# Attention scores of a pair of heads as 64-row products issued in turn into two banks

## The chip, the core and the metric

The kernel runs on one core of one Trainium2 chip. The metric is device time in microseconds (us) of one execution. Before the change it is 724.13 us, the median of three runs (723.54 to 724.2). The engines named below are TensorE (PE, with its weight loads as PEld), VectorE (DVE), ScalarE (ACT) and SyncE (SP), which issues the DMAs.

## The reference

One layer of a hybrid block over 512 latent tokens (a grid of 8 rows by 64 columns) and 256 context tokens, 1024 wide, 16 heads of 64. The change lies in branch B, a neighbourhood attention with all context keys in one softmax:

```python
s_nb = (jnp.einsum('bqhd,bpqjhd->bqhpj', q_r, k_win).astype(jnp.float32) * scale
        + jnp.transpose(bias, (1, 0, 2, 3))[None].astype(jnp.float32))
s_ctx = jnp.einsum('bqhd,bchd->bqhc', q_r, k_ctx).astype(jnp.float32) * scale
p = jax.nn.softmax(jnp.concatenate([s_nb, s_ctx], axis=-1), axis=-1).astype(v.dtype)
```

A score is a sum over the 64 channels of one head. Branch A (a gated short convolution), the projections, the gates, the merge and the output projection stand around it.

## The kernel before

All matrix operands are kept as two parts of type fp32r, a high part H (the rounded value) and a low part L (what rounding left), and a product of two matrices is a sum of three products, H·H + H·L + L·H (`step_T`, L115 to L117). `split` (L70, L71) makes the parts: the cast of H on ACT, the difference L on DVE.

The tokens are ordered by grid column, so that 512 queries fall into four blocks of 128, and a block's window keys are at most 256 of the 512 latent keys. With 256 context keys a block of one head has 512 scores, one bank of PSUM. Heads go in eight pairs (`p`); a pair fills 128 partitions, its first head the lower 64 (`lo`), its second the upper 64 (`hi`).

`keys_queries(p)` projects a pair's queries and keys and makes their parts. As a head has 64 channels only, the parts are doubled: for head h, `qd[h]` holds the high part of its queries in both halves of the partitions and `qe[h]` the low part in both; `ks[h]` holds the high part of its keys in its own half and the low part in the other. A product with 128 rows of `qd[h]` with `ks[h]` is then H·H + H·L, one of `qe[h]` with `ks[h]` is L·H + L·L. So `scores(p, h, b)` needs two products of 512 columns for a block (L552), or four of 256 in block 3, whose window keys lie apart (L561). It then adds the bias and takes the maximum on DVE (L568), the exponential with its sum on ACT (L574), the reciprocal (L575) and the scaling (L576).

`turn2` transposes the probabilities of two blocks of one head on PE (L583) and splits them into TH and TL. `gather(p, h, TH, TL)` multiplies them with the values (L599) and writes a head's 64 rows of `attn[p]`.

These steps are laid between projections that the rest of the layer needs: `plan` gives each pair its list, as generators that yield after 16 to 32 products. The last loop runs over 64 blocks (p, h, b); at each it takes the next pieces of fill, issues a finished head's gather, and issues the scores two blocks ahead. What stands in which order on an engine is then settled by a scheduler, which keeps to this order by and large.

Of eight PSUM banks the fill has three, the scores two (`psS`, one block each), the transposes two, the gather one. `bt` holds the bias of the two heads, loaded by SP at a head's first block; the 512 KB halves of the weight chunks (`raw`) go through the same queue. The last pieces are the gather of the last head and `gate2(3)`; after them the merge stage splits the conv branch (`us`) and the attention (`as`) and multiplies them with their output weights.

Of the kernel before, what the change touches and what calls it, by code (L numbers as in the profile page):

```python
# [9 lines left out]
F32 = mybir.dt.float32  # L10
F32R = mybir.dt.float32r
AF = mybir.ActivationFunctionType
ALU = mybir.AluOpType
AX = mybir.AxisListType

P = 128
D = 1024
KT = 8
S = 512
C = 256  # L20
EPS = 1e-6
NPAIR = 8
# [5 lines left out]
def layer(ctx: ExitStack, tc, xp, ctxt, ctxT, cc, wmod, small, wfirst, win, wout, wo, rel, tab, out):  # L28
    nc = tc.nc
# [25 lines left out]
    def pairs(tag, n, dtype=F32R):  # L55
        t = [hp.tile([P, 2, n], dtype, name=f"{tag}{k}") for k in range(KT)]
        return t, ([x[:, 0] for x in t], [x[:, 1] for x in t])
# [6 lines left out]
    _, hx = pairs("h", S)  # L64
    hcs, hc = pairs("hc", C)

    def split(H, L, src, scale=None):

        if scale is None:
            nc.scalar.copy(H, src)  # L70
            nc.vector.tensor_sub(L, src, H.bitcast(F32))  # L71
        else:
            nc.scalar.mul(H, src, scale)
            nc.vector.scalar_tensor_tensor(
                out=L, in0=src, scalar=scale, in1=H.bitcast(F32), op0=ALU.mult, op1=ALU.subtract
            )
# [152 lines left out]
    def unit(w, i, m=hx):  # L229
        ps = pj()  # L230
        proj_T(ps, w, i, m)
        return ps


    with ExitStack() as p0:
# [8 lines left out]
        tps = Banks(6, 7)  # L244
# [8 lines left out]
        cols = {}  # L253
# [61 lines left out]
        with tc.manual_schedule(engines={E.PE, E.DVE, E.Activation, E.SP}):  # L315
# [74 lines left out]
            for k in range(KT):  # L390
# [9 lines left out]
                m = st.tile([P, S], F32, name="m", bufs=2)  # L400
# [57 lines left out]
        ks = [5, 6, 7, 0, 1, 2, 3, 4]  # L458
# [13 lines left out]
    aw = pa.enter_context(tc.tile_pool(name="aw", bufs=2, reuse_waits="tile"))  # L472
    swap = [(i + 16) % 32 for i in range(32)]
    lo, hi = slice(0, 64), slice(64, P)
    psS, psT, psO = Banks(3, 4), Banks(5, 6), Banks(7)
    bt = aw.tile([P, 5, 256], F32, name="bt", bufs=1)
    nc.vector.memset(bt[:, 4], 0.0)
    V, KQ = {}, {}
# [30 lines left out]
    def keys_queries(p):  # L509
        w = chunk()  # L510
        qf = rope(unit(w, 0), 64)
        sc = 0.125
        qd = [aw.tile([P, S], F32R, name="qd", bufs=3) for h in range(2)]
        qe = [aw.tile([P, S], F32R, name="qe", bufs=3) for h in range(2)]
        for h, r in ((0, lo), (1, hi)):
            for o in (lo, hi):
                nc.scalar.mul(qd[h][o], qf[r], sc)  # L517
            for o in (lo, hi):
                nc.vector.scalar_tensor_tensor(
                    out=qe[h][o], in0=qf[r], scalar=sc, in1=qd[h][r].bitcast(F32), op0=ALU.mult, op1=ALU.subtract  # L520
                )
            if h == 0:
                yield
        ks = [aw.tile([P, S + C], F32R, name="ks", bufs=4) for h in range(2)]

        def keys(src, cols):
            for h, r, o in ((0, lo, hi), (1, hi, lo)):
                nc.scalar.copy(ks[h][r, cols], src[r])
                nc.vector.tensor_sub(ks[h][o, cols], src[r], ks[h][r, cols].bitcast(F32))

        keys(rope(unit(w, 1)), slice(0, S))
        yield
        ps = pj()
        proj_c(ps, w, 1)
        keys(summed(ps), slice(S, S + C))
        KQ[p] = qd, qe, ks
        yield

    def scores(p, h, b):
        qd, qe, ks = KQ[p]
        if b == 0:
            nc.sync.dma_start(bt[:, 2 * h:2 * h + 2], rel[p, h])
        s = psS()
        qs = slice(b * P, (b + 1) * P)
        if b < 3:

            t = ks[h][:, b * P:(b + 2) * P]
            kt = bass.AP(t.tensor, t.offset, [t.ap[0], [(4 - b) * P, 2], [1, 2 * P]])  # L550
            for n, lhs in enumerate((qd[h], qe[h])):
                nc.tensor.matmul(  # L552
                    s.rearrange("p (a c) -> p a c", a=2), lhsT=lhs[:, qs], rhs=kt, start=n == 0, stop=n == 1
                )
        else:
            kt = ks[h].rearrange("p (t c) -> p t c", c=P)
            s4 = s.rearrange("p (t c) -> p t c", c=P)
            n = 0
            for lhs in (qd[h], qe[h]):
                for o, i in ((slice(0, 2), slice(0, 4, 3)), (slice(2, 4), slice(4, 6))):  # L560
                    nc.tensor.matmul(  # L561
                        s4[:, o], lhsT=lhs[:, qs], rhs=kt[:, i], start=n == 0, stop=n == 3, skip_group_check=True
                    )
                    n += 1
        e = 2 * h + (b == 3)
        m = aw.tile([P, 1], F32, name="m", bufs=4)
        s3 = s.rearrange("p (a c) -> p a c", a=2)
        nc.vector.tensor_tensor_reduce(  # L568
            out=s3, in0=s3, in1=bt[:, e::4 - e][:, 0:2], scale=-1.0, scalar=3.0e38,
            op0=ALU.add, op1=ALU.min, accum_out=m,  # L570
        )
        pt = aw.tile([P, S], F32, name="pt", bufs=3)
        z = aw.tile([P, 1], F32, name="z", bufs=4)
        nc.scalar.activation(pt, s, AF.Exp, bias=m, scale=-1.0, accum_out=z)  # L574
        nc.vector.reciprocal(z, z)  # L575
        nc.scalar.mul(pt, pt, z)  # L576
        return pt

    def turn2(pts, b, TH, TL):
        tps = [psT().rearrange("p (c q) -> p c q", c=4) for _ in pts]  # L580
        for tp, pt in zip(tps, pts):
            for c in range(4):
                nc.tensor.transpose(tp[:, c], pt[:, c * P:(c + 1) * P], ident)  # L583
        for n, tp in enumerate(tps):
            split(TH[:, b + n], TL[:, b + n], tp)

    def gather(p, h, TH, TL):
        r, q = (lo, hi)[h], (hi, lo)[h]
        o = psO()
        o3 = o.rearrange("p (b q) -> p b q", b=4)  # L590

        work = [(4, slice(0, 4), lambda t: t[:, :, 2]), (5, slice(0, 4), lambda t: t[:, :, 3])]
        work.append((0, slice(0, 4, 3), lambda t: t[:, 0:4:3, 0]))
        for k in range(1, 3):
            work.append((k, slice(k - 1, k + 1), lambda t, k=k: t.rearrange("p b c q -> p (b c) q")[:, 4 * k - 3:4 * k + 1:3]))
        work.append((3, slice(2, 4), lambda t: t[:, 2:4, 1]))
        for n, (kt, dst, src) in enumerate(work):
            for t in (TH, TL):
                nc.tensor.matmul(  # L599
                    o3[:, dst], lhsT=V[p][:, kt, h], rhs=src(t),  # L600
                    start=n == 0 and t is TH, stop=n == len(work) - 1 and t is TL,
                )
        tmp = aw.tile([P, S], F32, name="tmp", bufs=1)
        nc.scalar.copy(tmp[r], o[q])
        nc.vector.tensor_add(attn[p][r, 64:512], o[r, :448], tmp[r, :448])
        nc.vector.tensor_add(attn[p][r, 0:64], o[r, 448:], tmp[r, 448:])
# [10 lines left out]
    def gate2(g):  # L617
        w = chunk()
        gate(2 * g, w, 0)
        yield  # L620
        gate(2 * g + 1, w, 1)
        yield
# [13 lines left out]
    def chain(*gs):  # L636
        for g in gs:
            yield from g
# [11 lines left out]
    for p in range(NPAIR):  # L650
        f = []
# [5 lines left out]
            }[name](i))  # L657
        fill.append(f)
    pj.tags = (0, 1, 2)
    blocks = [(p, h, b) for p in range(NPAIR) for h in range(2) for b in range(4)]  # L660
    pts = {n: scores(*blocks[n]) for n in range(2)}
    T = None
    done = 0
    for i, (p, h, b) in enumerate(blocks):
        slot = i % 8
        if slot == 0:
            items = chain(*(g for g, _ in fill[p]))
            total, done = sum(n for _, n in fill[p]), 0
        upto = -(-total * (slot + 1) // 8)
        while done < upto:  # L670
            next(items)
            done += 1
        if T is not None and b == 0:
            gather(*T)
        if i + 2 < len(blocks):
            pts[i + 2] = scores(*blocks[i + 2])
        if b == 0:
            TH = aw.tile([P, 4, 4, P], F32R, name="TH", bufs=1)
            TL = aw.tile([P, 4, 4, P], F32R, name="TL", bufs=1)
            T = p, h, TH, TL  # L680

        if b % 2:
            turn2([pts.pop(i - 1), pts.pop(i)], b - 1, TH, TL)
    gather(*T)
    for _ in gate2(3):
        pass
    pa.close()

# [4 lines left out]
    for n, srcs in (("u", u), ("a", attn)):  # L693
        t = [bp.tile([P, 2, S], F32R, name=f"{n}s{k}") for k in range(KT)]
# [48 lines left out]
    for j in range(KT):  # L743
        w = chunk()
        g = G[j]
        for i in range(2):
            nc.vector.scalar_tensor_tensor(  # L747
                out=g[i], in0=g[i], scalar=1.0, in1=unit(w, i, ua[i]), op0=ALU.add, op1=ALU.mult
# [8 lines left out]
        if j == 1 or j == 3:  # L757
            q = j // 2
# [9 lines left out]
        if j == 4:  # L768
# [4 lines left out]
            for i in range(2):  # L773
                gb = cv.tile([P, S], F32, name="ta")
                ps = pj()
                for k in range(4):
                    n = 4 * i + k
# [91 lines left out]
    for q in range(2):  # L869
        nc.vector.scalar_tensor_tensor(  # L870
            out=raws[q][:, :, h0], in0=raws[q][:, :, h0], scalar=-1.0, in1=raws[2 + q][:, :, h0],
            op0=ALU.mult, op1=ALU.subtract,
        )
        split(S4[q][:, 0], S4[q][:, 1], raws[q][:, :, h0])
    t = [hp.tile([P, 2, S], F32R, name=f"wB22{i}", tag=f"h{2 + i}") for i in range(4)]
# [25 lines left out]
    for i in range(2):  # L901
        cols = slice(256 * i, 256 * (i + 1))
# [92 lines left out]
```

## Time and profile before

| | |
|---|---|
| median of three runs | 724.13 us |
| the profiled execution, its time | 723.86 us |
| its span (first to last instruction) | 722.1 us |
| PE clock granted over the span | 0.999 |
| score products | 96 of 512 columns (L552), 64 of 256 (L561) |
| other products in the stage of the scores | transposes 256 (L583), gathers 192 (L599), the rest projections |
| DMA over the span | 86.63 MB, 120 GB/s |

The stage from the first score to the last gather lies between about 137 and 515 us of the span. In the rows shown later, a group's line gives the kernel's line, the engine, the operation, the tile written and those read, the shapes and the count, then busy time and mean duration in ns, and last the idle time of the engine before the group and what ended it. In a timeline a row has its start, its length and, in brackets, idle time and what ended it. A matmul's duration runs until its last result is written, and the next one starts earlier; so sums of durations are not time, and distances of starts are.

### The profile page before, as it was taken

The page shows a single profiled execution, that of the slowest core. Times are in us where ns is not written, and L with a number is a line of the kernel's source. Part 1 is how long each engine was busy: PE and PEld are TensorE (multiplying, and loading weights), DVE is VectorE, ACT ScalarE, POOL GpSimd, SP SyncE. Part 2 cuts the span into 40 slices and gives each one's busy share as a digit, 9 for nine tenths or more (in the row PEclk, how much of TensorE's full clock was granted, in tenths as well). Part 3 has the DMA queues.
Part 4 walks back from the last instruction along what each step waited for, and adds up shares of the span by engine and source line. Part 5 has one row for each costly group of instructions (what it writes and reads, how often), then busy time and mean ns, then how long its engine had stood idle before and what let it go on. Part 6 is the DMA issues. An engine that isn't in the chain of part 4 may idle for free.

```text
span 722.1 us, 9274 instructions
## 1 busy us (share of the span) xinstructions
PE 711.1 (98%) x3476; PEld 596.9 (83%) x3476; DVE 507.3 (70%) x955; ACT 392.8 (54%) x706; POOL 0.7 (0%) x6
## 2 busy tenths in 40 slices
PE   7999999999999999999999999999999999999996
PEld 4888888888888888888888888888888888888885
DVE  6979999794887848758768678565763333343997
ACT  6576533674676755755657647555742223133573
POOL 0000000000000000000000000000000000000000
PEclk9999999999999999999999999999999999999999
DMA  8985883213122122122321222222442322424103
GB/s 340 405 325 189 312 266 116 89 62 113 59 74 74 59 87 74 59 73 74 99 93 44 74 89 72 74 80 95 130 138 83 116 87 89 145 91 171 59 1 117
DMA packets 26543, 86.63 MB, mean 120 GB/s; under 512 B 3073, under 2 KB 3329, under 8 KB 26498
## 3 DMA queue, kind: packets, MB, share of 16 engines
q1 hardware_dynamic: 26354, 85.90, 35.1%
q8 instruction: 27, 0.44, 0.3%
q14 instruction: 18, 0.15, 0.1%
q10 hardware_dynamic: 144, 0.13, 0.1%
HBM read 83.93 MB, written 2.10 MB: 119 GB/s over the span
## 4 chain that ended last, share of the span: by engine, by line
PE 96%; DVE 1%; DMA 1%; SPq 0%; ACT 0%; issue 0%; DVEq 0%; ACTq 0%
PE ps L116 21%; PE ps L117 21%; PE ps L115 21%; PE ps L128 6%; PE ps L801 5%; PE ps L599 4%; PE ps L583 4%; PE ps L133 3%; PE ps L552 3%; PE ps L141 2%; PE ps L307 2%; PE ps L311 2%; PE ps L308 2%; DMA fraw<-in_wfirst 1%; PE ps L561 1%; PE ps L146 1%
## 5 line engine op out<-in xcount | busy, mean ns | idle before, releaser
L115 PE MATMUL ps<-h,w 128*128 128x512 f32 x528 | 207.6, 393 | 0.0
L117 PE MATMUL ps<-h,w 128*128 128x512 f32 x528 | 205.7, 390 | 0.0
L116 PE MATMUL ps<-h,w 128*128 128x512 f32 x528 | 205.7, 390 | 0.0
L71 DVE TENSOR_TENSOR w<-raw,w 128x1024 fp32r<-128x1024 f32 x90 | 107.8, 1218 | 49.1 <-ACT w L70 48.9
L70 ACT CAST w<-raw 128x1024 fp32r<-128x1024 f32 x90 | 92.0, 1050 | 72.5 <-PE ps L117 64.6
L117 PEld LDWEIGHTS ps<-h,w 128*128 128x128 f32 x528 | 99.1, 188 | 20.7
L116 PEld LDWEIGHTS ps<-h,w 128*128 128x128 f32 x528 | 99.2, 188 | 20.2
L115 PEld LDWEIGHTS ps<-h,w 128*128 128x128 f32 x528 | 99.2, 188 | 20.1
L574 ACT ACTIVATE pt<-ps,m 128x512 f32<-128x512 f32 x64 | 44.1, 690 | 32.2 <-DVE m L568 31.8
L576 ACT ACTIVATE pt<-pt,z 128x512 f32<-128x512 f32 x64 | 46.7, 731 | 13.9 <-DVE z L575 13.9
L568 DVE CUSTOM_DVE_ANT_1 ps<-ps,bt 128x512 f32<-128x512 f32 x56 | 38.6, 699 | 19.0 <-PE ps L552 14.6
L71 DVE TENSOR_TENSOR TL<-ps,TH 128x512 fp32r<-128x512 f32 x64 | 43.1, 682 | 10.3 <-ACT TH L70 10.3
L747 DVE SCALAR_TENSOR_TENSOR g<-g,ps 128x512 f32<-128x512 f32 x16 | 11.0, 687 | 39.9 <-PE ps L117 39.9
L632 ACT ACTIVATE g<-ps 128x512 f32<-128x512 f32 x16 | 9.6, 598 | 54.1 <-PE ps L117 54.1
L70 ACT CAST TH<-ps 128x512 fp32r<-128x512 f32 x64 | 35.6, 589 | 3.6 <-PE ps L583 3.4
L583 PE MATMUL ps<-ident,pt 128*128 128x128 f32 x256 | 33.4, 273 | 0.2 <-DVE TL L71 0.2
L128 PE MATMUL ps<-w,h 128*128 128x512 f32 x128 | 32.5, 394 | 0.0
L583 PEld LDWEIGHTS ps<-ident,pt 128*128 128x128 f32 x256 | 29.2, 141 | 2.8 <-issue 0.6
L599 PE MATMUL ps<-TH,V 128*128 128x256 f32 (+1 forms) x96 | 28.5, 319 | 0.0
L517 ACT ACTIVATE qd<-ta 64x512 fp32r<-64x512 f32 x32 | 20.2, 631 | 14.2 <-DVE ta L491 11.3
L599 PE MATMUL ps<-TL,V 128*128 128x256 f32 (+1 forms) x96 | 27.7, 318 | 0.0
L128 PEld LDWEIGHTS ps<-w,h 128*128 128x128 f32 x128 | 23.1, 189 | 4.2
(192 smaller groups left out, 1169.6 us busy)
## 6 DMA issues: line engine op xcount, KB each, us to landing
raw<-in_win SPq DMA_DIRECT2D x74, 512.0 KB, 4.2
wm<-in_wmod SPq DMA_DIRECT2D x34, 512.0 KB, 7.1
raw<-in_wout SPq DMA_DIRECT2D x16, 512.0 KB, 4.6
bt<-in_rel SPq DMA_DIRECT2D x16, 256.0 KB, 2.6
B<-in_wo SPq DMA_DIRECT2D x8, 512.0 KB, 7.2
fraw<-in_wfirst SPq DMA_DIRECT2D x8, 384.0 KB, 8.7
x<-in_xp SPq DMA_DIRECT2D x4, 512.0 KB, 5.2
xr<-in_xp SPq DMA_DIRECT2D x8, 256.0 KB, 3.0
```

The source lines that it names most:

```text
L70: nc.scalar.copy(H, src)
L71: nc.vector.tensor_sub(L, src, H.bitcast(F32))
L115: nc.tensor.matmul(ps, lhsT=H[:, k, cs], rhs=mH[k], start=k == 0, stop=False)
L116: nc.tensor.matmul(ps, lhsT=H[:, k, cs], rhs=mL[k], start=False, stop=False)
L117: nc.tensor.matmul(ps, lhsT=L[:, k, cs], rhs=mH[k], start=False, stop=k == KT - 1)
L128: nc.tensor.matmul(ps, lhsT=mH[k][:, ts], rhs=both[:, k].rearrange("p a c -> p (a c)"), start=k == 0, stop=False, skip_group_check=True,)
L568: nc.vector.tensor_tensor_reduce(out=s3, in0=s3, in1=bt[:, e::4 - e][:, 0:2], scale=-1.0, scalar=3.0e38, op0=ALU.add, op1=ALU.min, accum_o ...
L574: nc.scalar.activation(pt, s, AF.Exp, bias=m, scale=-1.0, accum_out=z)
L576: nc.scalar.mul(pt, pt, z)
L583: nc.tensor.transpose(tp[:, c], pt[:, c * P:(c + 1) * P], ident)
L599: nc.tensor.matmul(o3[:, dst], lhsT=V[p][:, kt, h], rhs=src(t), start=n == 0 and t is TH, stop=n == len(work) - 1 and t is TL,)
L801: nc.tensor.matmul(out, lhsT=a(x, k, ts), rhs=w[y][k // 2][:, k % 2, cols], start=start and k + o == 0, stop=k == 3 and o == 2, skip_group ...
```

## The change

A pair's queries and keys are split once, over all 128 partitions, into qH, qL and kH, kL. A block's scores are now taken for both heads of the pair at once: H·H, H·L and L·H, each as two products with 64 rows, the lower half for the first head into one bank, the upper half for the second into the other, in turn. Block 3 has them in two parts of 256 columns.

```diff
-        qd = [aw.tile([P, S], F32R, name="qd", bufs=3) for h in range(2)]
-        qe = [aw.tile([P, S], F32R, name="qe", bufs=3) for h in range(2)]
-        for h, r in ((0, lo), (1, hi)):
-            for o in (lo, hi):
-                nc.scalar.mul(qd[h][o], qf[r], sc)
...
+        qs = [aw.tile([P, S], F32R, name=n) for n in ("qH", "qL")]
+        split(*qs, qf, sc)
...
-            for h, r, o in ((0, lo, hi), (1, hi, lo)):
-                nc.scalar.copy(ks[h][r, cols], src[r])
-                nc.vector.tensor_sub(ks[h][o, cols], src[r], ks[h][r, cols].bitcast(F32))
+            split(ks[0][:, cols], ks[1][:, cols], src)
...
+    def load_bias(p, e):
+        nc.sync.dma_start(bt[:, e:4:2], rel[p, :, :, e].rearrange("h q c -> q h c"))
...
-    def scores(p, h, b):
-        qd, qe, ks = KQ[p]
+    def scores(p, b):
+        (qH, qL), (kH, kL) = KQ[p]
         if b == 0:
-            nc.sync.dma_start(bt[:, 2 * h:2 * h + 2], rel[p, h])
-        s = psS()
+            load_bias(p, 1)
+        ss = [psS() for h in range(2)]
...
+        parts = ((slice(0, 4), None),) if b < 3 else ((slice(0, 2), slice(0, 4, 3)), (slice(2, 4), slice(4, 6)))
+        n = 0
+        for q, k in ((qH, kH), (qH, kL), (qL, kH)):
+            for o, i in parts:
+                for h, r in enumerate((lo, hi)):
...
                     nc.tensor.matmul(
+                        dst, lhsT=q[r, qs], rhs=kt, start=n == 0, stop=n == 3 * len(parts) - 1, skip_group_check=True
                     )
...
+        if b == 2 and p + 1 < NPAIR:
+            load_bias(p + 1, 0)
...
-    def gather(p, h, TH, TL):
+    def gather(p, h):
+        TH, TL = T[h]
...
-    blocks = [(p, h, b) for p in range(NPAIR) for h in range(2) for b in range(4)]
+    blocks = [(p, b) for p in range(NPAIR) for b in range(4)]
+    T = [[aw.tile([P, 4, 4, P], F32R, name=f"T{n}{h}", bufs=1) for n in "HL"] for h in range(2)]
+    load_bias(0, 0)
+    ahead = scores(0, 0)
     for i, (p, b) in enumerate(blocks):
...
+            if p and b == 0:
+                gather(p - 1, h)
+            if h == 0 and i + 1 < len(blocks):
+                ahead = scores(*blocks[i + 1])
+        turn2(pts, b)
+    gather(NPAIR - 1, 0)
+    last = gate2(3)
+    next(last)
+    gather(NPAIR - 1, 1)
+    for _ in last:
         pass
```

Softmax, transposes and gathers stay as they were, two heads at a time: `turn2` takes one block of both heads, so a pair's TH and TL of both heads are kept until both gathers, which stand in the next pair's first block. The bias tile is loaded in two parts per pair, by kind of block (that of block 3, and that of the others) and not by head. The last gather stands between the two pieces of `gate2(3)`.

On PE at the start of the stage, before: the first two blocks of the first head, two products each (qd, qe: the doubled query parts; the number of ps names the bank's tile), then projections.

```order
L552 MATMUL ps_1303<-ks_1086,qd_1074 128x512
L552 MATMUL ps_1303<-ks_1086,qe_1076 128x512
L552 MATMUL ps_1313<-ks_1086,qd_1074 128x512
L552 MATMUL ps_1313<-ks_1086,qe_1076 128x512
L115 MATMUL ps_1332<-h0_80,w_1151 128x512
```

On PE at the same place, now: the first block of both heads.

```order
L554 MATMUL ps_1296<-kH_1078,qH_1074 128x512
L554 MATMUL ps_1297<-kH_1078,qH_1074 128x512
L554 MATMUL ps_1296<-kL_1079,qH_1074 128x512
L554 MATMUL ps_1297<-kL_1079,qH_1074 128x512
L554 MATMUL ps_1296<-kH_1078,qL_1075 128x512
L554 MATMUL ps_1297<-kH_1078,qL_1075 128x512
L115 MATMUL ps_1327<-h0_80,w_1139 128x512
```

Six products that change banks at each step stand where four stood that filled one bank after the other; the projections before and behind are the same.

On PE at block 3 of the first head, before: two parts of 256 columns for each of qd and qe, and then the transposes.

```order
L117 MATMUL ps_1391<-h7_87,w_1151 128x512
L561 MATMUL ps_1426<-ks_1086,qd_1074 128x256 x2
L561 MATMUL ps_1426<-ks_1086,qe_1076 128x256 x2
L583 MATMUL ps_1438<-ident_71,pt_1308 128x128 x4
L583 MATMUL ps_1439<-ident_71,pt_1318 128x128 x4
```

On PE at block 3 of the first pair, now: the high query part, with the two key parts, for both banks.

```order
L117 MATMUL ps_1528<-h7_87,w_1322 128x512
L554 MATMUL ps_1556<-kH_1078,qH_1074 128x256
L554 MATMUL ps_1557<-kH_1078,qH_1074 128x256
L554 MATMUL ps_1556<-kH_1078,qH_1074 128x256
L554 MATMUL ps_1557<-kH_1078,qH_1074 128x256
L554 MATMUL ps_1556<-kL_1079,qH_1074 128x256
L554 MATMUL ps_1557<-kL_1079,qH_1074 128x256
```

Six more of these follow, and then projections in place of the transposes.

At the end of the stage the last gather stood on PE behind the first four to seven products of `gate2(3)`; now it stands behind its first 24, with 24 more behind it.

More of the change, by code (lines that the diff above doesn't have):

```diff
@@ L512, in keys_queries @@
         sc = 0.125
-        qd = [aw.tile([P, S], F32R, name="qd", bufs=3) for h in range(2)]
-        qe = [aw.tile([P, S], F32R, name="qe", bufs=3) for h in range(2)]
-        for h, r in ((0, lo), (1, hi)):
-            for o in (lo, hi):
[L517 to L524, printed above, removed]
+        qs = [aw.tile([P, S], F32R, name=n) for n in ("qH", "qL")]
+        split(*qs, qf, sc)
+        yield
+        ks = [aw.tile([P, S + C], F32R, name=n) for n in ("kH", "kL")]
         def keys(src, cols):
-            for h, r, o in ((0, lo, hi), (1, hi, lo)):
-                nc.scalar.copy(ks[h][r, cols], src[r])
-                nc.vector.tensor_sub(ks[h][o, cols], src[r], ks[h][r, cols].bitcast(F32))
+            split(ks[0][:, cols], ks[1][:, cols], src)
         keys(rope(unit(w, 1)), slice(0, S))
@@ L535, in keys_queries @@
         keys(summed(ps), slice(S, S + C))
-        KQ[p] = qd, qe, ks
+        KQ[p] = qs, ks
         yield
-    def scores(p, h, b):
-        qd, qe, ks = KQ[p]
+    def load_bias(p, e):
+        nc.sync.dma_start(bt[:, e:4:2], rel[p, :, :, e].rearrange("h q c -> q h c"))
+    def scores(p, b):
+        (qH, qL), (kH, kL) = KQ[p]
         if b == 0:
-            nc.sync.dma_start(bt[:, 2 * h:2 * h + 2], rel[p, h])
-        s = psS()
+            load_bias(p, 1)
+        ss = [psS() for h in range(2)]
@@ L546, in scores @@
         qs = slice(b * P, (b + 1) * P)
[L547 to L560, printed above, removed]
+        parts = ((slice(0, 4), None),) if b < 3 else ((slice(0, 2), slice(0, 4, 3)), (slice(2, 4), slice(4, 6)))
@@ new lines, in scores @@
+        n = 0
+        for q, k in ((qH, kH), (qH, kL), (qL, kH)):
+            for o, i in parts:
+                for h, r in enumerate((lo, hi)):
+                    if b < 3:
+                        t = k[r, b * P:(b + 2) * P]
+                        kt = bass.AP(t.tensor, t.offset, [t.ap[0], [(4 - b) * P, 2], [1, 2 * P]])
+                        dst = ss[h].rearrange("p (a c) -> p a c", a=2)
+                    else:
+                        kt = k[r].rearrange("p (t c) -> p t c", c=P)[:, i]
+                        dst = ss[h].rearrange("p (t c) -> p t c", c=P)[:, o]
@@ L561, in scores @@
                     nc.tensor.matmul(
-                        s4[:, o], lhsT=lhs[:, qs], rhs=kt[:, i], start=n == 0, stop=n == 3, skip_group_check=True
+                        dst, lhsT=q[r, qs], rhs=kt, start=n == 0, stop=n == 3 * len(parts) - 1, skip_group_check=True
                     )
[L564 to L579, printed above, removed]
+                n += 1
+        pts = []
+        for h, s in enumerate(ss):
+            e = 2 * h + (b == 3)
+            m = aw.tile([P, 1], F32, name="m", bufs=4)
+            s3 = s.rearrange("p (a c) -> p a c", a=2)
+            nc.vector.tensor_tensor_reduce(
+                out=s3, in0=s3, in1=bt[:, e::4 - e][:, 0:2], scale=-1.0, scalar=3.0e38,
+                op0=ALU.add, op1=ALU.min, accum_out=m,
+            )
+            pt = aw.tile([P, S], F32, name="pt", bufs=4)
+            z = aw.tile([P, 1], F32, name="z", bufs=4)
+            nc.scalar.activation(pt, s, AF.Exp, bias=m, scale=-1.0, accum_out=z)
+            nc.vector.reciprocal(z, z)
+            nc.scalar.mul(pt, pt, z)
+            pts.append(pt)
@@ L580, in turn2 @@
+        if b == 2 and p + 1 < NPAIR:
+            load_bias(p + 1, 0)
+        return pts
+    def turn2(pts, b):
         tps = [psT().rearrange("p (c q) -> p c q", c=4) for _ in pts]
@@ L583, in turn2 @@
                 nc.tensor.transpose(tp[:, c], pt[:, c * P:(c + 1) * P], ident)
-        for n, tp in enumerate(tps):
-            split(TH[:, b + n], TL[:, b + n], tp)
-    def gather(p, h, TH, TL):
+        for tp, (TH, TL) in zip(tps, T):
+            split(TH[:, b], TL[:, b], tp)
+    def gather(p, h):
+        TH, TL = T[h]
         r, q = (lo, hi)[h], (hi, lo)[h]
@@ L659, in layer @@
     pj.tags = (0, 1, 2)
-    blocks = [(p, h, b) for p in range(NPAIR) for h in range(2) for b in range(4)]
[L661 to L666, printed above, removed]
+    blocks = [(p, b) for p in range(NPAIR) for b in range(4)]
+    T = [[aw.tile([P, 4, 4, P], F32R, name=f"T{n}{h}", bufs=1) for n in "HL"] for h in range(2)]
+    load_bias(0, 0)
+    ahead = scores(0, 0)
+    for i, (p, b) in enumerate(blocks):
+        if b == 0:
             items = chain(*(g for g, _ in fill[p]))
             total, done = sum(n for _, n in fill[p]), 0
[L669 to L685, printed above, removed]
+        pts = ahead
+        for h in range(2):
+            upto = -(-total * (2 * b + h + 1) // 8)
+            while done < upto:
+                next(items)
+                done += 1
+            if p and b == 0:
[8 more added lines that the diff above has]
+    for _ in last:
         pass
```

## The prediction

> **What bounds the kernel now.** I read the page's first part (busy time of each engine) and its fourth (the chain that ended last) first.
>
> ```profile
> PE 711.1 (98%) x3476; PEld 596.9 (83%) x3476; DVE 507.3 (70%) x955; ACT 392.8 (54%) x706; POOL 0.7 (0%) x6
> PE 96%; DVE 1%; DMA 1%; SPq 0%; ACT 0%; issue 0%; DVEq 0%; ACTq 0%
> ```
>
> TensorE (PE) is busy 98% of the span and makes up 96% of the chain. "Busy" counts the tail of a product too, so the stage that the change touches, from the first score to the last gather, is read next, in a view of engine busy time by stretch and in the list of waits of that stretch.
>
> ```profile
> 137.00:515.00 378.00, 377.83 (x1978) 322.82 (x1977) 270.80 (x583) 237.86 (x461) 0.00 (x0) 1.00 0.23 74
> PEld ps L583 <- DVE TL L71: 0.2, 1, 0.2
> ```
>
> In those 378 us PE (first figure after the length) lacks 0.17 us, and its one wait for an elementwise engine in the list is 0.2 us. VectorE (DVE) is busy 271 us and ScalarE (ACT) 238 us of 378. So in this stage time is the sum of PE's products at the pace at which they follow each other; nothing that DVE, ACT or a DMA saves there can give more than 0.2 us. The pace is not the duration in the groups (0.39 us, in which the pipeline's tail is counted) but the distance of starts. The chain in order of time shows it:
>
> ```profile
> 137.15 0.93 PE ps L552 x4
> 138.07 0.23 PE ps L115
> ...
> 149.41 0.47 PE ps L561 x4
> 149.88 0.87 PE ps L583 x8
> ```
>
> Four score products of 512 columns take 0.93 us, as much per product (0.23) as a projection product of L115; four of 256 columns take 0.47 (0.1175 each). A product is paid by its columns here; all of these use 128 rows.
>
> **The change, term by term.** The groups with shapes kept apart give the counts.
>
> ```profile
> L552 PE MATMUL ps<-ks,qe 128*128 128x512 f32 x48 | 18.9, 395 | 0.0
> L552 PE MATMUL ps<-ks,qd 128*128 128x512 f32 x48 | 18.8, 393 | 0.0
> L561 PE MATMUL ps<-ks,qe 128*128 128x256 f32 x32 | 6.4, 283 | 0.0
> L561 PE MATMUL ps<-ks,qd 128*128 128x256 f32 x32 | 6.4, 281 | 0.0
> ```
>
> *A, the streams.* Before: 96 x 0.23 + 64 x 0.1175 = 22.1 + 7.5 = 29.6 us. After, for each of 8 pairs of heads: three blocks of 3 couples of 512 columns and one block of 6 couples of 256, a couple being the same product of the lower and of the upper 64 rows. If the two of a couple stream at the same time, that is 72 x 0.23 + 48 x 0.1175 = 16.6 + 5.6 = 22.2 us: **-7.4**. If they stream one after the other, it is twice that, 44.4: **+14.8**. No row of this case shows two products in the array at once, and these are the two ends. I take the overlap: a couple shares no row of the array, no partition of its operands and no bank.
>
> *B, the switches.* Each of the 32 blocks goes from products of 128 rows to products of 64 and back: 64 switches. The trace has one change of row count, at its start, where products with one row (L355) are followed by products with 128 (L364). Start, duration, then what ran:
>
> ```profile
> 5.19 0.33 PEld L355 LDWEIGHTS ps<-crow,ones 1*128 1x128 f32 x1 [0.52 <-issue]
> 5.19 1.06 PE L355 MATMUL ps<-crow,ones 1*128 1x512 f32 x1
> 5.43 0.59 ACT L359 COPY cb<-ps 128x512 f32<-128x512 f32 x1 [0.65 <-PE ps L355]
> 6.04 1.06 PE L355 MATMUL ps<-crow,ones 1*128 1x512 f32 x1
> 7.03 0.29 PEld L364 LDWEIGHTS ps<-cb,ident 128*128 128x128 f32 x1 [1.50 <-issue]
> 7.03 0.80 PE L364 MATMUL ps<-cb,ident 128*128 128x256 f32 x1
> 7.62 0.63 PE L364 MATMUL ps<-cb,ident 128*128 128x256 f32 x1
> 8.07 0.48 PE L387 MATMUL ps<-ident,x 128*128 128x128 f32 x1
> ```
>
> Within one row count a weight load (PEld) starts as the product before it starts: 5.19 and 5.19. The load of L364 could have started at 6.04 in the same way: its operand was written by the copy that ended at 6.02. It started at 7.03, when the last one-row product was about to end (7.10), with nothing that the profile shows to wait for. So at a change of row count the array emptied first. The delay there: L364 starts 0.99 after its predecessor where 0.85 was the pace (5.19 to 6.04), and its next pass follows after 0.59 where the one after takes 0.45: 0.14 + 0.14 = 0.28 us. The products ran slowly there. At the pace of the stage I rebuild it from a duration and a restart:
>
> ```profile
> 15.44 0.19 PEld L307 LDWEIGHTS ps<-h,fH 128*128 128x128 f32 x1 [1.60 <-ACT h L70]
> 15.44 0.50 PE L307 MATMUL ps<-h,fH 128*128 128x512 f32 x1 [1.20 <-ACT h L70]
> 15.54 0.19 PEld L308 LDWEIGHTS ps<-h,fL 128*128 128x128 f32 x1
> 15.77 0.39 PE L308 MATMUL ps<-h,fL 128*128 128x512 f32 x1
> ```
>
> After an empty array the next product starts 0.33 after the first and not 0.23, so an uncovered load costs 0.10. With the tail 0.39 - 0.23 = 0.16, less the 0.07 by which the load came ahead of the end (7.10 - 7.03), a switch costs 0.16 - 0.07 + 0.10 = 0.19, say 0.20 us: **64 x 0.20 = +12.8**. Ends: 0, if 64 rows need no emptying, and 64 x 0.28 = 17.9. I take 0.20, from rows at the stage's own pace.
>
> The Trainium skill, "TensorEngine Tiling (Array Packing)", section "Key Properties", says that changing the tiling mode, not just the tile, drains TensorE. It speaks against this change, and the trace agrees for its one switch: 7.03 in place of 6.04. By that rule the sum keeps B; without it B would be zero.
>
> *C, the loads.* A couple needs two weight loads where one product needed one. The two loads above start 0.10 apart (15.44, 15.54), one after the other. If loads of the two halves also go in turn, the upper half starts 0.10 late in each block, 32 x 0.10 = 3.2, and a couple of 256 columns lasts two loads, 0.20, in place of 0.1175: 48 x 0.08 = 4.0. Together 7.2; if the halves load at the same time, 0. Couples of 512 columns (0.23) hide two loads either way. Loads to different halves have no row here, so neither end is nearer; I take the middle, **+3.6**.
>
> The Trainium skill, "TensorE: Matmul & The Clock Gate", section "Part 3: Packing small matmuls", says that a load overlaps products in flight where its row group differs, and that products of different tiles start some 4 ns apart. By it C would be 0 and the time 729.3; no run here shows it yet.
>
> *Priced at nothing.* The query and key parts are no longer doubled:
>
> ```profile
> L519 DVE SCALAR_TENSOR_TENSOR qe<-ta,qd 64x512 fp32r<-64x512 f32 x32 | 21.9, 686 | 1.2 <-ACT qd L517 0.6
> L517 ACT ACTIVATE qd<-ta 64x512 fp32r<-64x512 f32 x32 | 20.2, 631 | 14.2 <-DVE ta L491 11.3 <-PE ps L561 2.6
> L529 DVE TENSOR_TENSOR ks<-ta,ks 64x512 fp32r<-64x512 f32 x16 | 11.0, 686 | 0.5
> L528 ACT CAST ks<-ta 64x512 fp32r<-64x512 f32 x16 | 9.9, 618 | 2.1 <-DVE ta L487 1.9
> L70 ACT CAST TH<-ps 128x512 fp32r<-128x512 f32 x64 | 35.6, 589 | 3.6 <-PE ps L583 3.4
> L71 DVE TENSOR_TENSOR TL<-ps,TH 128x512 fp32r<-128x512 f32 x64 | 43.1, 682 | 10.3 <-ACT TH L70 10.3
> ```
>
> A cast of 128 rows (0.59 on ACT, 0.68 on DVE) costs no more than one of 64 (0.62 and 0.69). So ACT loses 24 of the 32 query casts and 8 of the 16 key casts, about 24 x 0.63 + 8 x 0.62 = 20 us, and DVE about 22 (casts of the 256 context columns apart). PE hid all of it (0.2 us of waits in the stage), so it buys nothing.
>
> The bias loads of a pair are cut differently but stay 16, of 256 KB:
>
> ```profile
> SPq L544 <- DVE m L568: 113.4, 13, 14.3
> bt<-in_rel SPq DMA_DIRECT2D x16, 256.0 KB, 2.6
> ```
>
> The queue (SP) waits 113 us in all for the reductions that free the bias tile, and PE never felt it, though the weight loads stand behind them. The new order keeps that: 0.
>
> A block now takes both banks, so the next block waits until both heads' softmax have read them:
>
> ```profile
> L568 DVE CUSTOM_DVE_ANT_1 ps<-ps,bt 128x512 f32<-128x512 f32 x56 | 38.6, 699 | 19.0 <-PE ps L552 14.6 <-PE ps L561 4.2
> L574 ACT ACTIVATE pt<-ps,m 128x512 f32<-128x512 f32 x64 | 44.1, 690 | 32.2 <-DVE m L568 31.8
> ```
>
> The tail 0.16, two reductions of 0.70 and the second exponential of 0.69 are about 2.3 us. Between two blocks of the new order PE has at least 24 projection products, 5.5 us, and mostly 8 to 12. Covered: 0.
>
> At the stage's end the last gather moves behind one gate unit, and the u splits stand on ACT behind its copy:
>
> ```profile
> 515.18 0.58 ACT L604 COPY tmp<-ps 64x512 f32<-64x512 f32 x1 [1.04 <-PE ps L599]
> 516.59 3.10 DVE L71 TENSOR_TENSOR us<-u,us 128x512 fp32r<-128x512 f32 x5
> ```
>
> From that copy to the first u split (3.10 / 5 = 0.62 each) were 516.59 + 0.62 - 515.18 = 2.0 us. After the last gather PE has 24 products of the last gate, 5.5 us, before one needs a u split, and then takes three products, 0.69, for each further one. Covered: 0.
>
> Sum: -7.4 + 12.8 + 3.6 = **+9.0** on the profiled execution's own 723.86 us (span 722.1 and 1.8 around it): **732.9**. The median of the runs, 724.13, lies 0.04% beside it.
>
> **Rivals.** *Overlap without switches' cost* (faster): the array takes 64-row products among 128-row ones without emptying. For it: the one switch seen is from one row, not 64. Against: the 0.99 us in which a load with nothing to wait for did not start. -7.4 gives 716.5; with loads in turn, up to 723.7.
>
> *No overlap* (the change does not do what it says): the couple streams in turn. For it: every start in the trace follows its predecessor by a full stream. Against: nothing in it had rows to spare. +14.8 gives 738.7 without switch costs, 751.5 with 12.8.
>
> *A new wait for the banks*: the softmax chain of 2.3 us meets queued weight splits, two on DVE and two on ACT.
>
> ```profile
> L71 DVE TENSOR_TENSOR w<-raw,w 128x1024 fp32r<-128x1024 f32 x90 | 107.8, 1218 | 49.1 <-ACT w L70 48.9
> L70 ACT CAST w<-raw 128x1024 fp32r<-128x1024 f32 x90 | 92.0, 1050 | 72.5 <-PE ps L117 64.6
> ```
>
> It then takes 2.3 + 2.4 + 2.1 = 6.8 us. That decides where the distance between two blocks is shorter: the new order has three such, 5.5, 6.4 and 6.4 us by these paces, so 1.3 + 0.4 + 0.4 = 2.1 us more, 735.0. Against: those two engines had 107 and 140 us to spare.
>
> **How the numbers follow.** The sign hangs on one point: A gives 7.4 us, and 64 switches use that up from 0.116 us each. Forecast (overlap, emptying) 0.53, with a range of its own from -7.4 + 64 x 0.09 = 722.3 (only the tail, the load hidden) to -7.4 + 17.9 + 7.2 = 741.6. Overlap without switch cost 0.23; no overlap 0.17, of which 0.10 with the switches; the banks 0.07. A measurement of this kernel can tell about 0.2% from no change, 1.4 us. Faster: 0.20 of the second case and 0.02 of the forecast's low end, 0.22. Same: 0.03 and 0.04, 0.07. Slower: 0.71. The range 715.5 to 745 leaves out the 0.10 at 751.5 and the edges of the others.
>
> **What would show it.** In the new profile, starts of the two products of a couple: well under 0.23 apart means overlap, 0.23 means none. The first load of a block: at its predecessor's start means no emptying, some 0.32 after it means B; likewise the first product behind a block. Loads of the two halves at one time, or 0.10 apart, settle C, best in the blocks of 256 columns. PE waiting for an exponential at a block's first product would be the third rival. From the start of the product before a block of 512 columns to the start of the one behind it, now 5 x 0.23 = 1.15 us, the forecast has 1.15 - 0.23 + 0.40 = 1.32, or 1.42 with loads in turn. It is wrong if that is under 1.1 (no emptying) or over 1.6 (no overlap).

## The result and the profile after

The changed kernel takes 728.82 us, the median of four runs (728.75 to 729.36), against 724.16 us of before: a ratio of 1.0068, with a 95% interval of 1.005 to 1.0085. In a later comparison it was 729.24 against 723.66, 1.0078 (1.0065 to 1.009). It is slower by 4.7 to 5.6 us. The profiled execution has a span of 727.5 us where before had 722.1: 5.4 more.

First the page of the changed kernel, busy time by engine and the chain's shares:

```profile
PE 716.8 (99%) x3556; PEld 589.6 (81%) x3556; DVE 484.8 (67%) x915; ACT 365.8 (50%) x666; POOL 0.7 (0%) x6
PE 96%; DMA 1%; ACT 1%; DVE 1%; SPq 0%; issue 0%; DVEq 0%; ACTq 0%
```

DVE lost 22.5 us of work and ACT 27.0, and PE is still the chain: none of it came back. The stage, in the view of busy time by stretch, and PE's waits in the whole span:

```profile
137.00:521.00 384.00, 383.94 (x2057) 315.64 (x2056) 252.12 (x548) 214.05 (x426) 0.00 (x0) 1.00 0.23 75
PE ps L355 <- ACT crow L327: 3.3, 1, 3.3
PE ps L307 <- ACT h L70: 1.2, 1, 1.2
```

PE has no gap there, and both its waits lie at the start of the span, as before. The new order made no wait. So the 5.4 us are in the distances of products. The timeline of one block, products and weight loads (start, duration):

```profile
143.25 0.39 PE L116 MATMUL ps<-h,w 128*128 128x512 f32 x1
143.26 0.19 PEld L117 LDWEIGHTS ps<-h,w 128*128 128x128 f32 x1
143.48 0.39 PE L117 MATMUL ps<-h,w 128*128 128x512 f32 x1
143.80 0.19 PEld L554 LDWEIGHTS ps<-kH,qH 64*128 64x128 f32 x2 [0.35 <-issue]
143.80 0.50 PE L554 MATMUL ps<-kH,qH 64*128 64x512 f32 x2
143.91 0.19 PEld L554 LDWEIGHTS ps<-kL,qH 64*128 64x128 f32 x2
144.13 0.40 PE L554 MATMUL ps<-kL,qH 64*128 64x512 f32 x2
144.14 0.19 PEld L554 LDWEIGHTS ps<-kH,qL 64*128 64x128 f32 x2
144.37 0.40 PE L554 MATMUL ps<-kH,qL 64*128 64x512 f32 x2
144.69 0.19 PEld L115 LDWEIGHTS ps<-h,w 128*128 128x128 f32 x1 [0.37 <-issue]
144.70 0.50 PE L115 MATMUL ps<-h,w 128*128 128x512 f32 x1
145.03 0.40 PE L116 MATMUL ps<-h,w 128*128 128x512 f32 x1
```

Three things are to be read here. A row of L554 holds two products, one of each half, and ends no later than one of them would (0.40, as a single product of 512 columns): they run at the same time; their starts in the trace are 3 to 4 ns apart. Two loads in a row of 0.19 show the same for the weights. And the first load of the block is not pulled ahead: the load for L117 starts at 143.26 with the product before it (143.25), the one for L554 at 143.80, 0.32 after L117 started and 0.07 before that product's end, with "issue", nothing to wait for, in brackets. The load of the first product behind (144.69) does the same after the last couple (144.37). Both are the switch of the prediction.

From L117 (143.48) to the second product behind the block (145.03) are 1.55 us; with the pace of 0.23 for five steps it would be 1.15. The difference, 0.40, is two switches of 0.20.

### The profile page after: what moved, and what is told of

Same layout as the page of the kernel before. It is cut to its first block, busy times and chain, and to the rows that moved or that the text cites. A ratio compares the mean times of both kernels' runs of the same rounds, so it can differ in the third digit from the quotient of the medians.

```text
span 727.5 us, 9305 instructions
## 1 busy us (share of the span) xinstructions
PE 716.8 (99%) x3556; PEld 589.6 (81%) x3556; DVE 484.8 (67%) x915; ACT 365.8 (50%) x666; POOL 0.7 (0%) x6
## 4 chain that ended last, share of the span: by engine, by line
PE 96%; DMA 1%; ACT 1%; DVE 1%; SPq 0%; issue 0%; DVEq 0%; ACTq 0%
PE ps L115 21%; PE ps L117 21%; PE ps L116 20%; PE ps L128 6%; PE ps L798 5%; PE ps L598 4%; PE ps L554 4%; PE ps L581 4%; PE ps L133 3%; PE ps L141 2%; PE ps L307 2%; PE ps L311 2%; PE ps L308 2%; DMA fraw<-in_wfirst 1%; PE ps L146 1%; PE ps L300 0%
## 5 line engine op out<-in xcount | busy, mean ns | idle before, releaser
L117 PE MATMUL ps<-h,w 128*128 128x512 f32 x528 | 205.8, 390 | 0.0
L117 PEld LDWEIGHTS ps<-h,w 128*128 128x128 f32 x528 | 99.1, 188 | 21.3
L571 ACT ACTIVATE pt<-pt,z 128x512 f32<-128x512 f32 x64 | 43.1, 719 | 1.4 <-DVE z L570 1.3
L603 ACT COPY tmp<-ps 64x512 f32<-64x512 f32 x16 | 9.3, 581 | 43.1 <-PE ps L598 43.0
L153 DVE TENSOR_TENSOR ta<-ta,ps 128x256 f32<-128x256 f32 x32 | 13.4, 421 | 23.4 <-ACT ta L152 23.4
```

Of the source, the lines that this page charges most:

```text
L117: nc.tensor.matmul(ps, lhsT=L[:, k, cs], rhs=mH[k], start=False, stop=k == KT - 1)
```

## Experiments

Each kernel below is the changed one with the edit shown (`...` stands for what is left out). Its time stands beside that of before on the same chip. A *run* is a row of 64-row products with no 128-row product among them; it has two switches, its way in and its way out.

**Order and banks without 64-row products.** Two products of all 128 rows per head and block.

```diff
-        for q, k in ((qH, kH), (qH, kL), (qL, kH)):
+        for q, k in ((qH, kH), (qL, kH)):
...
-                        t = k[r, b * P:(b + 2) * P]
+                        t = k[:, b * P:(b + 2) * P]
...
-                        dst, lhsT=q[r, qs], rhs=kt, start=n == 0, stop=n == 3 * len(parts) - 1, skip_group_check=True
+                        dst, lhsT=q[:, qs], rhs=kt, start=n == 0, stop=n == 2 * len(parts) - 1, skip_group_check=True
```

> The changed kernel with two products of 128 rows per head and block in place of three of 64 rows (high and low query part with the high key part; the sum then runs over the channels of both heads and leaves the low key part out, so the scores are others). Same order, banks, casts and bias loads as the changed kernel, as many products as before (96 of 512 columns, 64 of 256), no change of row count. Theory (each change of row count empties the array, 64 times 0.20 us; nothing else of the change costs or gives time): 723.9, within 0.7 us of before. Rival (the new order, the two banks taken at once or the bias loads cost the difference): 727 or more.

Measured: 723.13 against 723.87 (ratio 0.9991, 0.9982 to 1.0). That is 0.74 us below before, just outside the expected margin of 0.7. Taken together, the new order, the banks taken two at a time, the undoubled casts and the other cut of the bias loads cost nothing, and the 22 to 27 us that DVE and ACT were spared buy no more than the interval allows, 1.3 us. The rival is out.

**Six products of 128 rows.** The same edit, but with all three products per head kept, as in the changed kernel.

> The changed kernel with all six products per block taken over 128 rows (the sum runs over the channels of both heads, so the scores are others); order, banks, casts and the number of products stay. Theory (products of 128 rows stream one after the other, and no switch is paid): 29.6 us of score streams become 44.4, so before + 14.8 = 738.9, within 1.5. Rival (the cost found lies in the number of products and loads or in changing banks at each product, not in the row count): those 14.8 and another 5 to 13 us, 744 or more.

Measured: 738.47 against 723.87, +14.6. Where products use all rows, 240 stream one after the other at the price of 160 plus half, and nothing else is paid. The chain, in order of time, has the block:

```profile
143.90 0.23 PE ps L117
144.13 1.36 PE ps L554 x6
145.49 0.23 PE ps L115
```

Six products in turn over two banks take 1.36 us, 0.23 each, and the projection behind follows without a gap. So neither the number of loads nor the change of banks makes the switch; the row count does.

**Both products of a couple in one half.**

```diff
-                for h, r in enumerate((lo, hi)):
+                for h, r in enumerate((lo, lo)):
```

> The changed kernel with both products of a couple taken from the lower 64 rows (the second head's scores are then the first's); everything else as in the changed kernel. Theory (products overlap because they lie in different halves of the rows, and the 64 switches stay): the streams of 22.2 us become 44.4, so 728.8 + 22.2 = 751.0, within 2. Rival (short products of 64 rows are cheaper for another reason, such as their loads or the two banks): nearer to 728.8 than to 751.

Measured: 751.24 against 723.66; the changed kernel on the same chip had 729.24, so +22.0. Same switches, same loads, same banks, and the overlap is gone:

```profile
144.37 0.73 PE L554 MATMUL ps<-kH,qH 64*128 64x512 f32 x2
144.94 0.63 PE L554 MATMUL ps<-kL,qH 64*128 64x512 f32 x2
145.41 0.62 PE L554 MATMUL ps<-kH,qL 64*128 64x512 f32 x2
145.96 0.50 PE L115 MATMUL ps<-h,w 128*128 128x512 f32 x1
```

From the second row to the third are 0.47 us, two streams, where the changed kernel has 0.24. The overlap is worth 22 us. This kernel also prices the switch by itself: it streams as many products one after the other as the one of 128 rows before it (240) and differs from it in the row count, and its profiled span is 749.2 against 736.5, 12.7 us more, 0.20 for each of 64 switches.

**The halves one after the other.** Three (or six) products of the lower half are issued first.

```diff
-        for q, k in ((qH, kH), (qH, kL), (qL, kH)):
-            for o, i in parts:
-                for h, r in enumerate((lo, hi)):
+        for h, r in enumerate((lo, hi)):
+            n = 0
+            for q, k in ((qH, kH), (qH, kL), (qL, kH)):
+                for o, i in parts:
...
-                n += 1
+                    n += 1
```

> The changed kernel with the three (six in block 3) products of the lower half first and then those of the upper half, not in turn; 64 switches stay. Theory (two products overlap only where neighbours in the queue use different halves): a block of 512 columns takes 5 streams of 0.23 in place of 3, one of 256 columns 11 of 0.1175 in place of 6: 24 x 0.46 + 8 x 0.59 = +15.8 on 728.8, so 744.6, within 2. Rival (the halves are filled from the queue whatever the order): 728.8, unchanged.

Measured: 731.88 against 723.87; beside the changed kernel's 728.8 to 729.2 only some 3 us more. The theory missed by 13. A block of 512 columns, in the timeline:

```profile
143.42 0.39 PE L117 MATMUL ps<-h,w 128*128 128x512 f32 x1
143.74 0.50 PE L554 MATMUL ps<-kH,qH 64*128 64x512 f32 x2
144.07 0.40 PE L554 MATMUL ps<-kL,qH 64*128 64x512 f32 x2
144.31 0.40 PE L554 MATMUL ps<-kH,qL 64*128 64x512 f32 x2
144.64 0.50 PE L115 MATMUL ps<-h,w 128*128 128x512 f32 x1
```

Each half has only one product of kH with qH here, so the row "kH,qH x2" is the first and the fourth of the queue: the fourth started (10 ns after the first) before the second and the third. In block 3, with six products ahead of it, the upper half came late:

```profile
166.86 0.50 PE L554 MATMUL ps<-kH,qH 64*128 64x256 f32 x2
167.20 0.28 PE L554 MATMUL ps<-kL,qH 64*128 64x256 f32 x1
167.21 0.38 PE L554 MATMUL ps<-kH,qH 64*128 64x256 f32 x1
167.32 0.28 PE L554 MATMUL ps<-kL,qH 64*128 64x256 f32 x1
```

The two kH,qH of the lower half start in the first row; the upper half's first is at 167.21, with the lower half's third (167.20), when three of the lower half were still in front of it. Block 3 got 0.35 us longer, eight times 2.8, which is the 3 us. So the halves are fed past each other, but only over a few products.

**Two runs per block: more switches.** H·H and H·L in one place, L·H a piece of fill later.

```diff
-        for q, k in ((qH, kH), (qH, kL), (qL, kH)):
+        for q, k in ((qH, kH), (qH, kL), (qL, kH))[some[0]:some[1]]:
...
-            if h == 0 and i + 1 < len(blocks):
-                ahead = scores(*blocks[i + 1])
+            if i + 1 < len(blocks):
+                if h == 0:
+                    ss = [psS() for _ in range(2)]
+                scores(*blocks[i + 1], ss, (0, 2) if h == 0 else (2, 3))
+                if h == 1:
+                    ahead = softmax(*blocks[i + 1], ss)
```

> The changed kernel with each block's products in two runs, H.H and H.L first, L.H after the next piece of fill where there is one: 56 runs in place of 32, so 112 switches; the products are the same and as many. Theory (0.40 us per run, 0.35 where transposes follow): 728.8 + 24 x 0.40, less 0.05 for some 18 more runs that end on transposes: 737.5, within 1.5. Rival (the cost goes with the products or with the first load of a bank): 729 to 730.

Measured: 739.16 against 723.94, a span of 737.5: 10.0 us over the changed kernel's profiled span for 24 more runs, 0.42 each. It is 1.7 over the expected 737.5, just outside the margin. Most of that is a wait for a bank, which the list of PE's waits does not show, as the other half was streaming meanwhile:

```profile
245.53 0.19 ACT L571 ACTIVATION_READ_ACCUMULATOR pt<-ps,m 128x1 f32 x1
245.54 0.73 PE L553 MATMUL ps<-kH,qH 64*128 64x512 f32 x2
245.88 0.62 PE L553 MATMUL ps<-kL,qH 64*128 64x512 f32 x2
246.43 0.50 PE L115 MATMUL ps<-h,w 128*128 128x512 f32 x1
```

The first couple takes 0.73 in place of 0.50: its upper half started 0.23 after the lower, at 245.77, 0.05 after an exponential (L571, with the read of its sum) had ended. In the program that product waits for ACT. Six runs are like this, each with the same 0.05, and each is longer by 0.23: 1.4 us. The other 8.6 are 0.36 for each of the 24 runs; all 24 end on transposes (31 runs do here, 7 in the changed kernel), where the expectation had 0.35 for them.

**Two blocks per run: fewer switches.** Four banks of scores at once; scores, transposes and gathers share five banks in turn.

```diff
-    psS, psT, psO = Banks(3, 4), Banks(5, 6), Banks(7)
+    psS = psT = psO = Banks(3, 4, 5, 6, 7)
...
-    blocks = [(p, b) for p in range(NPAIR) for b in range(4)]
+    blocks = [(p, b) for p in range(NPAIR) for b in (0, 2)]
...
+            if h == 1:
+                turn2(pts[0], b)
+            if h == 2 and more:
+                ss = [scores(q, c + n) for n in range(2)]
+                ahead.append(softmax(q, c, ss[0]))
...
```

> The changed kernel with the scores of two blocks issued together, so that 16 runs of 64-row products stand where 32 stood: 32 switches in place of 64. Scores, transposes and gathers share five banks in turn for it. Theory (0.20 us per switch): 728.8 - 6.4 = 722.4, below before. Rival (the cost goes with each product of 64 rows, not with the switch): 728.8 or more. Sharing the banks could add waits of PE on either theory; they would be listed as waits.

Measured: 730.04 against 723.87 (1.0085, 1.0072 to 1.0099). That reads like the rival, but the list of waits has a row that the changed kernel lacks:

```profile
PE ps L584 <- ACT pt L572: 6.0, 7, 1.0
```

L584 is the transposes there. The seven waits between transposes, counted as distances of starts beyond the pace, add to 7.7 us, and 728.8 - 6.4 + 7.7 = 730.1. Where a pair's list of fill left a place empty, the transposes stood directly behind four new banks of scores, and with their own two that is six where there are five. So the same was laid out, with the same banks, with fill between every run and the next transposes:

```diff
...
+            if h == 0:
+                if p and b == 0:
+                    gather(p - 1, 0)
+                    gather(p - 1, 1)
+                turn2(pts[0], b)
+            if h == 1 and more:
+                ss = [scores(q, c + n) for n in range(2)]
+                ahead.append(softmax(q, c, ss[0]))
...
```

> Scores of two blocks issued together as in the run before this one, but with projections between every score run and the next transposes, and both gathers of a pair put before the first of them: 16 runs of 64-row products, 32 switches. Theory (0.20 us per switch; the loss of the run before this one was transposes waiting for a bank or for probabilities): no wait of PE for an exponential in the list, 728.8 - 16 x 0.40 = 722.4, up to 723.0 because fewer runs end on transposes, where the way back is 0.05 shorter. Rival (taking four banks at once costs as much as the switches save, wherever it is put): 728 or more.

Measured: 723.25 against 723.94 (0.999, 0.9981 to 0.9999), 0.25 over the upper end of what was expected. No wait for an exponential is left among PE's, and the span is 721.1: 6.4 under the changed kernel for 16 runs fewer, 0.40 each. Its scores in the timeline:

```profile
150.80 0.50 PE L554 MATMUL ps<-kH,qH 64*128 64x512 f32 x2
151.14 0.40 PE L554 MATMUL ps<-kL,qH 64*128 64x512 f32 x2
151.37 0.40 PE L554 MATMUL ps<-kH,qL 64*128 64x512 f32 x2
151.61 0.40 PE L554 MATMUL ps<-kH,qH 64*128 64x256 f32 x4
151.85 0.40 PE L554 MATMUL ps<-kL,qH 64*128 64x256 f32 x4
152.08 0.40 PE L554 MATMUL ps<-kH,qL 64*128 64x256 f32 x4
```

Only the first couple takes 0.34 to its successor; the second block goes on at the pace, 0.24 for a couple of 512 columns or two of 256.

The changed kernel and this version were then put on one chip with before:

> The changed kernel itself, for a comparison on one chip with before and with the two-block version. 728.8 by what was measured; no theory differs here.

> The two-block version with spaced transposes again, on the same chip as the changed kernel. Theory (16 runs fewer at 0.40 us): the changed kernel less 6.4, less up to 0.4 fewer for ends on transposes: 5.5 to 6.4 below it, and 0.5 to 1.2 us below before.

Measured: 729.24 and 723.21, with before at 723.66. The two-block version is 6.0 us below the changed kernel and 0.45 below before (0.5 to 1.2 was expected), with an interval (0.9985 to 1.0003) that includes no difference. It undoes the loss; that it beats before is not shown, as the interval just excludes no difference in the one comparison and includes it in the other.

**Scores straight behind transposes.**

```diff
-    ahead = scores(0, 0)
+    ahead = [scores(0, 0), scores(0, 1)]
...
-        pts = ahead
+        pts = ahead.pop(0)
...
-            if h == 0 and i + 1 < len(blocks):
-                ahead = scores(*blocks[i + 1])
         turn2(pts, b)
+        if i + 2 < len(blocks):
+            ahead.append(scores(*blocks[i + 2]))
```

> The changed kernel with each block's scores issued straight behind the transposes of the block two before it, as many runs as before (32). Theory (each run pays both ways, whatever stands beside it): 728.8, within 0.7. Rival (the empty array behind transposes, where the second product starts 0.31 and not 0.23 after the first, is the same emptying, and next to each other the two are paid once): 32 x 0.09 to 0.14 less, 724.3 to 726.0.

Measured: 731.27 against 723.94, over what either expected. The rival is out: a block behind transposes pays its way in in full.

```profile
174.72 0.82 PE L581 MATMUL ps<-ident,pt 128*128 128x128 f32 x6
175.47 0.50 PE L554 MATMUL ps<-kH,qH 64*128 64x512 f32 x2
175.81 0.39 PE L554 MATMUL ps<-kL,qH 64*128 64x512 f32 x2
```

The first transpose of the row starts 5 paces of 0.109 before the last, at 175.27; the couple comes 0.20 after that, 0.09 over the pace, and its successor 0.34 after it, another 0.10: 0.19 as elsewhere. The 0.31 behind transposes, on which the rival rested, is no emptying: the first product there is recorded 0.08 early, 28 ns after the last transpose, and the two distances add up to the pace. Of the 2.4 us over the changed kernel, 0.35 is that all 32 runs end on projections where 7 had ended on transposes (0.05 cheaper), and 1.3 are two blocks near the beginning whose banks came free late. The loads' waits name the exponential:

```profile
PEld ps L554 <- ACT pt L569: 0.8, 2, 0.5
```

From the product before the block to the second behind it, the block at 141.00 took 0.85 more than its like in the changed kernel, its halves one after the other, and block 3 at 204.33 took 0.47 more than the others of its kind. The rest lies in part outside the stage and was not traced.

## Why the prediction came out as it did

*Bound by PE's pace: right.* Sparing DVE and ACT over 22 us each gave nothing that the interval shows (first experiment), and the whole change in span is in the distances of products. (The list that the prediction read has a second small wait, 0.3 us of a weight load for ACT; it changes nothing in the sum.)

*A, -7.4 us by overlap: right.* The couples run at one time, and taking the overlap away cost 22.0 us where the sum has 44.4 - 22.2 = 22.2.

*B, 64 switches of 0.20: right, in size too.* Way in and way out leave their loads uncovered. Two kernels that stream 240 products one after the other, with and without the 64 switches, differ by 12.7 us. Three kernels with 16, 32 and 56 runs have spans of 721.1, 727.5 and 737.5: 0.40 us per run of two switches between the first two, and between the last two 0.36, with the 1.4 us of bank waits taken off, for runs that end on transposes. Carried back to no run, 721.1 - 16 x 0.40 = 714.7 is 7.4 under before's span, which is A. That the emptying seen between one row and 128 holds between 64 and 128 was the weak point of the argument; it holds. The distance that the prediction named as a sign, from the product before a block to the first one behind it, is 1.22 us (143.48 to 144.70) and not 1.32: the last 0.10, the uncovered load of the way out, falls between the first and the second product behind. The total of 0.40 holds, its place was off. The rule of the Trainium skill cited in the prediction ("TensorEngine Tiling (Array Packing)", section "Key Properties"), that a change of tiling mode drains TensorE, agrees with all of this.

*C, +3.6 for loads in turn: mis-sized, it is 0.* The loads of the halves run at the same time (rows of two loads in 0.19), and block 3's couples follow at 0.117. The Trainium skill, "TensorE: Matmul & The Clock Gate", section "Part 3: Packing small matmuls", has loads of different row groups overlap, and these rows agree. I had put the middle between 0 and 7.2, because the only loads in the trace, of one row group, came 0.10 apart. Without C the sum is 723.86 - 7.4 + 12.8 = 729.3, and the profiled span grew by just that, 5.4. So of the forecast's +9.0 the missing 3.6 is this term alone.

*Covered terms: right.* No wait for banks, bias or the last gather appears in the changed kernel. That the bank rival is real showed in three of the variants: in the first two-block version, where six banks are asked for and five are there, in the one with two runs per block (1.4 us) and in the one with scores behind transposes (1.3 us).

*Rivals.* Overlap without switch costs and no overlap are both out. The break-even given there, 0.116 us per switch, lies well under the 0.20 measured.

## What to carry to other kernels

Splitting a product over halves of the rows pays only if the products of that kind come in long runs: here each run costs 0.40 us (in and out), a couple saves 0.23 against two products in turn, and with 32 runs the gain of 7.4 us was overpaid by 5.4. Count the runs before the products, and join runs if banks allow; then check that what shares those banks does not come right behind. A price that a trace shows only for another case (one row here, loads of one group) is worth a bound on each side, and the sum by each.

## What was not expected of the hardware

Products of different halves are not kept in the order of the queue: the fourth started before the second and third, 10 ns after the first, and, in block 3, over three waiting products but not over four or more of them. Why three, no run here shows. The Trainium skill, "TensorE: Matmul & The Clock Gate", section "Part 3: Packing small matmuls", has products start and end strictly in order; these rows differ, and the measurement decides. It follows that issuing the halves in turn, which the change took care to do, is needed only beyond a run of about three products in one half (three of 512 columns and six of 256 were tried, nothing between).
